# Attention on one core: transposing the weights of two units in a row, head 0's mixes at fixed places, a later v, and an earlier logarithm

## The chip, the cores and the metric

The kernel runs on one core of one Trainium2 chip. The metric is the device time of one execution in microseconds; before the change the median of three runs is 965.65 us (965.34 to 966.77). The engines are named as in the profile: PE is TensorE, with PEld for its weight loads; DVE is VectorE, ACT is ScalarE, POOL is GpSimd, SP is SyncE, which only issues DMAs here.

## What is computed

One layer of a decoder: 1,024 tokens of width 1,024, in float32. A norm, one wide projection, then two groups of heads side by side: eight heads of differential softmax attention and four of gated linear attention (GLA); their outputs are gated, multiplied by the output weights, normed and added to the input. The change touches the attention heads:

```python
s = jnp.einsum('bqhmd,bkhmd->bhmqk', qb, k)     # two maps m per head, 64 wide
p = jax.nn.softmax(jnp.where(mask, s, -jnp.inf), axis=-1)
w = p[:, :, 0] - lam * p[:, :, 1]
out = jnp.einsum('bhqk,bkhv->bqhv', w, v)
...
oa = rms_norm(oa, subln_g) * (1.0 - lam_init)
oa = oa.reshape(B, S, DA_WIDTH) * jax.nn.silu(ga)
```

## The kernel before, in words

Products in float32 are made of three matmuls on values split in a high and a low part (hi·hi, lo·hi, hi·lo); a cast on ACT gives the high part and a subtraction on DVE the low one. The program has three parts. Up to about 617 us stand the projections and GLA. From there to about 925 us comes attention. Then the finishing part adds up the output, norms it and stores it.

Attention is three streams of work, written as generators that `merge` (L1203) interleaves by costs written down in the code. All matmuls and transpositions are recorded by `mm` (L141, its instruction on L142) and `tr` (L144, L145) with `keep_in_program_order`, so the merged order is TensorE's order. The instructions of the other engines all carry L66, a helper; their order in each queue is chosen by the compiler's scheduler, unless an instruction is kept in program order or told to be issued after another (`issue_after`). A queue runs strictly in its order.

- `all_scores` (L1330) goes over the heads, and in a head over the query blocks qb from 7 down to 0, each of 128 queries and (qb+1)·128 keys. `scores` (L1263) does a block: for each map m, PE writes scores into one of three PSUM banks `sc` (up to 512 keys a part, two matmuls each: k and ks); DVE adds the mask, copies the part into the tile p and keeps the row's lowest (a reduction, CUSTOM_DVE_ANT_0, and an accumulator read); when a map's parts are in, ACT takes the exponential of the whole row and its sum. After both maps DVE takes the two reciprocals at once, POOL scales map 1 by lam and its reciprocal, and DVE mixes the two maps into p0 (SCALAR_TENSOR_TENSOR). That mix is the weight block. p0 of each block has a place of its own; p1 has two buffers for all of them, in the pool `smp`. In head 0 the mixes of blocks 7 to 4 are put off: a list holds them until the next block's second map is reduced.
- `all_values` (L1424) goes over units (head, half, keys): ten a head. `turn` (L1350) makes three or four transpositions of 128x128 into one of two PSUM banks `wtr` and takes the result out, ACT as `wt_hi`, DVE as `wt_lo` (three buffers each). `weigh` (L1366) multiplies with v into the bank `po`. Turns run two units ahead of weighs. After each half, `attn_norm` (L1380) norms the 128x512 output `o` and gates it: the squares, a matmul with ones (`ms`), logarithm and exponential on ACT, `r`; in head 7 the result `gate` stays on the chip for the end.
- `out_early` (L1528) makes the output's products that don't depend on what is still missing (`ypart`, three matmuls of 512 columns a step) and so fills TensorE between the other two.

`load_qk` (L1118) and `load_v` (L1238) issue DMAs on SP. Head 0's v is loaded ahead of the stream, by `v_first` (L1248), so the tile v has the first memory of `smp`. The projections store q and k with DMAs `q_d<-qk_st` (L482) from memory that `smp` takes over. At the end, `early_ends` (L1622) uses head 7's last gate: `last_part` (L1505) splits it into `m_hi` and `m_lo`, and `mix_pair` (L1612) had split the parts before (`m_raw`) behind the last square sums (`squared_last`).

Of the kernel before, what the change touches and what calls it, by code (L numbers as in the profile page):

```python
# [10 lines left out]
AF = mybir.ActivationFunctionType  # L11
# [9 lines left out]
DA_HEADS = 8  # L21
# [10 lines left out]
def hymba_kernel(  # L32
# [21 lines left out]
    pe, sp = nc.tensor, nc.sync  # L54
# [20 lines left out]
    act, dve, pool = Queue(nc.scalar), Queue(nc.vector), Queue(nc.gpsimd)  # L75

    def fp(t):
        return t.bitcast(F32)
# [37 lines left out]
    v_d = [tc.dram_tile([4, 2, P, NT, P], F32, name=f"v{u}_d") for u in range(2)]  # L116
# [1121 lines left out]
    def load_v(h):  # L1238
        v = [smp.tile([P, NT, P], F32R, tag="v", name=f"v{t}", bufs=4) for t in range(2)]
        for t in range(2):  # L1240

            with tc.issue_after(qk_load[0]) if h else nullcontext():
                ins = sp.dma_start(fp(v[t]), v_d[h // 4][h % 4, t])
            if h == 0:
                tc.keep_in_program_order(ins)
        return v

    v_first = load_v(0)  # L1248

    n_sc, n_tr = [0], [0]  # L1250

# [11 lines left out]
    def scores(h, qb):  # L1263

        n = (qb + 1) * P
        qc = slice(qb % 4 * P, qb % 4 * P + P)
        st = const.tile([P, 6], F32, tag="stt", name="stt", bufs=4)
        p0 = pp.tile([P, n], F32, tag=f"p0_{qb}", name="p0", bufs=1 + (qb > 5))
        p1 = smp.tile([P, S], F32, tag="p1", name="p1", bufs=2)
        for m, p in enumerate((p0, p1)):  # L1270
            q = qk[h, "q", qb // 4][:, m, qc]
            parts = parts_of(n)
            if h == DA_HEADS - 1 and (qb, m) in ((1, 1), (0, 0), (0, 1)):

                parts = [(0, 512)]
            for i, (a, b) in enumerate(parts):
                sc = sc_bank("sc", [P, 512])
                for j, name in enumerate(("k", "ks")):
                    for half in range(2):
                        lo, hi = max(a, half * 512), min(b, half * 512 + 512)  # L1280
                        if lo < hi:
                            mm(
                                sc[:, lo - a : hi - a], q,
                                qk[h, name, half][:, m, lo - half * 512 : hi - half * 512],
                                start=(j == 0), stop=(j == 1),
                            )
                e = min(b, n)
                last = i == len(parts) - 1

                behind = tc.issue_after(lowest[0]) if (h, qb) == (0, NT - 2) else nullcontext()  # L1290
                with behind:
                    ins = dve.tensor_tensor_reduce(
                        p[:, a:e], sc[:, : e - a],
                        maskt[:, NZ + P - (e - a) :] if last else maskt[:, : e - a],
                        1.0, 3e38 if i == 0 else st[:, 4 + m : 5 + m], ALU.add, ALU.min,
                        st[:, m : m + 1] if last else st[:, 4 + m : 5 + m],
                    )
                if (h, qb) == (0, NT - 1):
                    lowest[:] = [ins.ins]
                c = 0.08 + (e - a) / 512 * 0.56  # L1300
                if last:
                    act.activation(
                        p[:, :n], p[:, :n], AF.Exp, bias=st[:, m : m + 1], scale=-1.0,
                        accum_out=st[:, 2 + m : 3 + m],
                    )
                if last and m:
                    dve.reciprocal(st[:, 4:6], st[:, 2:4])
                    pool.tensor_scalar(
                        p1[:, :n], p1[:, :n], st[:, 5:6], lam, ALU.mult, ALU.mult
                    )  # L1310
                    while mixed:
                        with tc.issue_after(ins.ins):
                            mixed.pop()()

                    def mix_maps():
                        dve.scalar_tensor_tensor(
                            p0[:, :n], p0[:, :n], st[:, 4:5], p1[:, :n], ALU.mult, ALU.subtract
                        )
                        w[h, qb] = p0

                    if h == 0 and qb > 3:
                        mixed.append(mix_maps)
                    else:
                        mix_maps()
                    c += 0.25 + n / 1024 * 1.4
                yield c

    lowest, mixed = [], []

    def all_scores():  # L1330
        for h in range(DA_HEADS):
            for qb in range(NT - 1, -1, -1):
                if qb in (3, 5) and h:
                    yield lambda h=h, half=qb // 4: (h - 1, half) in used
                yield from scores(h, qb)
                if qb == 4 and h + 1 < DA_HEADS:
                    for n in ("q", "k", "ks"):
                        load_qk(h + 1, n, 1)
                    for n in ("k", "ks"):
                        load_qk(h + 1, n, 0)  # L1340
            if h + 1 < DA_HEADS:
                load_qk(h + 1, "q", 0)
        scored.append(True)
        opened.update(dict.fromkeys(SC))
# [5 lines left out]
    def turn(h, half, kts):  # L1350

        pt = tr_bank("wtr", [P, 512])
        n = 0
        for kt in kts:
            for i in blocks_of(kt, half):
                tr(pt[:, n : n + P], w[h, 4 * half + i][:, kt * P : (kt + 1) * P])
                n += P
        hi = smp.tile([P, 512], F32R, tag="wt_hi", name="wt_hi", bufs=3)
        lo = smp.tile([P, 512], F32R, tag="wt_lo", name="wt_lo", bufs=3)
        turned_last[:] = [act.copy(hi[:, :n], pt[:, :n]).ins]  # L1360
        dve.tensor_tensor(lo[:, :n], pt[:, :n], fp(hi[:, :n]), ALU.subtract)
        return hi, lo
# [14 lines left out]
                )  # L1377
            n += ns

    def attn_norm(h, half, o):  # L1380
        if h < DA_HEADS - 1:
            gate = smp.tile([P, 512], F32, tag="gate", name="gate", bufs=2)
        else:
# [10 lines left out]
        with tc.issue_after(turned_last[0]) if ending else nullcontext():  # L1394
            act.activation(sq[:64], o[:64], AF.Square)
        dve.tensor_tensor(sq[:64], sq[:64], fold[:64], ALU.add)
        ins = act.copy(hl[:64], sq[:64]).ins
        if ending:
            squared_last.append(ins)
        dve.tensor_tensor(hl[64:], sq[:64], fp(hl[:64]), ALU.subtract)  # L1400
        if h == DA_HEADS - 1:

# [7 lines left out]
            opened[TR[n_tr[0] % 2]] = None  # L1410
        r = smp.tile([P, 512], F32, tag="r", name="r", bufs=1)
        act.activation(r, ms, AF.Ln, bias=eps_t, scale=1.0 / P)
        act.activation(r, r, AF.Exp, scale=-0.5)
        if h < DA_HEADS - 1:
            dve.scalar_tensor_tensor(r, o, sub_g, r, ALU.mult, ALU.mult)
            pool.tensor_tensor(gate, r, gate, ALU.mult)
# [7 lines left out]
    def all_values():  # L1424


        AHEAD = 2
        units = [
            (h, half, kts) for h in range(DA_HEADS) for half in (1, 0)
            for kts in [(k,) for k in range(4 * half + 2)] + [(4 * half + 2, 4 * half + 3)]  # L1430
        ]
        vs, os, turned, norms_todo = {0: v_first}, {}, {}, []
        ahead = iter(units)

        def norm_step():
            while norms_todo:
                c = next(norms_todo[0], None)
                if c is not None:
                    return
                norms_todo.pop(0)  # L1440

        for i, (h, half, kts) in enumerate(units):
            last = kts[-1] == 4 * half + 3

            ahead_by = AHEAD if h < DA_HEADS - 1 else AHEAD
            while len(turned) < min(i + 1 + ahead_by, len(units)):
                u = next(ahead)
                if u[2] == (0,):
                    yield lambda: (u[0], 4 * u[1]) in w
                turned[u] = turn(*u)  # L1450
                if u[2][-1] == 4 * u[1] + 3:
                    used.add(u[:2])
                yield 0.4
                norm_step()
            if kts == (0,):
                o = smp.tile([P, 512], F32, tag="o", name="o", bufs=3)
                po = bank(PO, [P, 512], "po")
            weigh(po, half, kts, vs[h], turned[h, half, kts])
            norm_step()
            if last:  # L1460
                act.copy(o, po)
                if half and h + 1 < DA_HEADS:
                    vs[h + 1] = load_v(h + 1)
                norms_todo.append(attn_norm(h, half, o))
            yield 0.6

            if i == 1:
                yield SOON * DA_HEADS * 10.0 / T
        carry = norms_todo[-1]
        while len(norms_todo) > 1:  # L1470
            norm_step()
        next(carry)
        yield 0.0
        yield lambda: (ENDS[2], 0) in ps_d
        early_ends()
        yield from carry
# [319 lines left out]
```

## Time and profile before

| what | value |
|---|---|
| median of three runs | 965.65 us (965.34 to 966.77) |
| the profiled execution's own time | 964.64 us |
| its span, first to last instruction | 962.9 us |
| busy: PE, DVE, ACT, POOL | 953.0, 736.6, 603.6, 199.0 us |
| granted TensorE clock, mean | 0.998 |
| transpositions `wtr` | 288, busy 44.5 us |
| DMA | 220.36 MB, mean 229 GB/s |

Busy time is the share of time in which an engine had an instruction under way. Matmuls overlap, and their recorded ends are modelled, so what one costs TensorE is read between the starts of two in a row, not from its duration. In a timeline the columns are start, duration, engine, line, operation, output <- inputs, shapes, the count of equal instructions in the row, and in brackets how long the engine stood idle before it and what ended that.

### The profile page before, as it was taken

How to read it: one execution, taken by the hardware profiler on the slowest of the kernel's cores; microseconds unless marked ns; L12 is line 12 of the kernel's file. 1: busy time of each engine (PE TensorE's matmuls, PEld its weight loads, DVE VectorE, ACT ScalarE, POOL GpSimd, SP SyncE). 2: the span in 40 equal slices, each digit the busy share in tenths (PEclk: the TensorE clock that was granted, in tenths of full speed). 3: DMA queues.
4: the chain of work that ended last, by engine and by line, in shares of the span. 5: the costliest groups of instructions: out<-in, count | busy, mean ns of one | idle time of the engine just before them, and what ended most of it. 6: DMA issues, size and time to landing. Idle time of an engine off the chain costs nothing.

```text
span 962.9 us, 14404 instructions
## 1 busy us (share of the span) xinstructions
PE 953.0 (99%) x4640; PEld 795.9 (83%) x4640; DVE 736.6 (76%) x1468; ACT 603.6 (63%) x1166; POOL 199.0 (21%) x264
## 2 busy tenths in 40 slices
PE   9999999999999999999999999999999999999997
PEld 7887788888888888888888888878888888888875
DVE  5898799996678687687667576587888888898554
ACT  8753355845677556577765344366777787787773
POOL 3101002122142112111100002122222222433321
PEclk9999999999999999999999999999999999999999
DMA  9616367487577897985754498996666669994767
GB/s 343 217 35 167 91 196 253 163 299 246 189 251 239 281 309 236 299 285 193 259 175 145 151 291 273 408 305 198 219 207 208 220 226 357 320 292 104 162 196 149
DMA packets 152827, 220.36 MB, mean 229 GB/s; under 512 B 15728, under 2 KB 85360, under 8 KB 152656
## 3 DMA queue, kind: packets, MB, share of 16 engines
q1 hardware_dynamic: 138304, 177.65, 57.5%
q0 software_dynamic: 14448, 41.79, 14.9%
q8 instruction: 37, 0.61, 0.3%
q14 instruction: 38, 0.31, 0.1%
HBM read 133.93 MB, written 88.60 MB: 231 GB/s over the span
## 4 chain that ended last, share of the span: by engine, by line
PE 96%; ACT 1%; DVE 1%; DMA 1%; issue 0%; SPq 0%; DVEq 0%; ACTq 0%
PE x L142 24%; PE y L142 16%; PE z L142 16%; PE ypart L142 13%; PE sc L142 7%; PE po L142 5%; PE yps L142 4%; PE wtr L145 3%; PE gpo L142 3%; PE kv L142 1%; PE gkl_ps L142 1%; PE pa L142 1%; DMA x<-in_x_dram 1%; PE xT L145 1%; DVE p L66 1%
## 5 line engine op out<-in xcount | busy, mean ns | idle before, releaser
L66 ACT CAST w<-w_raw 128x512 fp32r<-128x512 f32 x138 | 85.2, 621 | 76.8 <-PE y L142 33.6
L66 DVE TENSOR_TENSOR w<-w_raw,w 128x512 fp32r<-128x512 f32 x138 | 94.1, 685 | 38.4 <-ACT w L66 38.2
L66 ACT ACTIVATE p<-p,stt 128x896 f32<-128x896 f32 (+7 forms) x128 | 99.3, 776 | 34.3 <-DVE stt L66 33.0
L66 ACT COPY s<-x 128x512 f32<-128x512 f32 x78 | 44.8, 587 | 74.2 <-PE x L142 74.0
L66 DVE CUSTOM_DVE_ANT_0 p<-sc,maskt 128x512 f32<-128x512 f32 (+3 forms) x128 | 74.3, 585 | 16.0 <-PE sc L142 14.6
L66 POOL TENSOR_SCALAR p<-p,stt,lam 128x1024 f32<-128x1024 f32 (+3 forms) x64 | 56.4, 882 | 144.8 <-DVE stt L66 144.1
L142 PE MATMUL z<-s_hi,w 128*128 128x512 f32 x320 | 80.2, 393 | 0.0
L142 PE MATMUL x<-s_hi,w 128*128 128x512 f32 x320 | 80.1, 392 | 0.0
L142 PE MATMUL y<-h_hi,w 128*128 128x512 f32 x320 | 80.1, 392 | 0.0
L142 PE MATMUL ypart<-wo_hi,m_hi 128*128 128x512 f32 x192 | 79.5, 414 | 0.1
L142 PE MATMUL ypart<-wo_hi,m_lo 128*128 128x512 f32 x192 | 75.5, 393 | 0.0
L142 PE MATMUL ypart<-wo_lo,m_hi 128*128 128x512 f32 x192 | 75.4, 393 | 0.0
L66 POOL DMA_DIRECT2D wo_d<-wo_hi x32 | 17.4, 544 | 275.0 <-ACT wo_hi L66 275.0
L142 PEld LDWEIGHTS z<-s_hi,w 128*128 128x128 f32 x320 | 59.8, 188 | 12.4
L142 PEld LDWEIGHTS x<-s_hi,w 128*128 128x128 f32 x320 | 59.7, 188 | 12.4
L142 PEld LDWEIGHTS y<-h_hi,w 128*128 128x128 f32 x320 | 59.7, 188 | 12.3
L142 PE MATMUL sc<-k,q 128*128 128x512 f32 (+1 forms) x192 | 68.7, 362 | 0.6 <-DVE stt L66 0.6
L142 PE MATMUL sc<-ks,q 128*128 128x512 f32 (+1 forms) x192 | 66.1, 347 | 0.0
L66 ACT CAST wt_hi<-wtr 128x512 fp32r<-128x512 f32 (+1 forms) x80 | 42.8, 535 | 27.1 <-PE wtr L145 26.1
L66 DVE TENSOR_TENSOR wt_lo<-wtr,wt_hi 128x512 fp32r<-128x512 f32 (+1 forms) x80 | 50.6, 632 | 9.0 <-ACT wt_hi L66 8.5
L66 DVE TENSOR_TENSOR w_raw<-w_raw 128x512 f32<-128x512 f32 x80 | 55.2, 690 | 1.2 <-DMA w_raw<-in_w_in_dram 0.2
L66 DVE TENSOR_TENSOR c<-z,s 128x512 f32<-128x512 f32 x48 | 32.8, 687 | 29.8 <-ACT s L66 19.9
(232 smaller groups left out, 2352.0 us busy)
## 6 DMA issues: line engine op xcount, KB each, us to landing
w_raw<-in_w_in_dram SPq DMA_DIRECT2D x40, 512.0 KB, 5.0
wo_d<-wo_hi POOLq DMA_DIRECT2D x32, 256.0 KB, 3.3
q<-q_d SPq DMA_DIRECT2D x32, 256.0 KB, 4.8
k<-k_d SPq DMA_DIRECT2D x32, 256.0 KB, 5.4
ks<-k_d SPq DMA_DIRECT2D x64, 128.0 KB, 5.9
v<-v_d SPq DMA_DIRECT2D x16, 512.0 KB, 6.5
wo_raw<-in_w_out_dram POOLq DMA_DIRECT2D x31, 256.0 KB, 4.8
wo_d<-gqd POOLq DMA_DIRECT2D x22, 256.0 KB, 4.2
```

The costliest lines, as they stand in the source:

```text
L66: ins = op(*a, **k)
L142: tc.keep_in_program_order(pe.matmul(*a, **k))
L145: tc.keep_in_program_order(pe.transpose(dst, src, ident))
```

## The change

It has five parts, all in attention.

1. **Turns in pairs.** `turn` only transposes; the take-out is a function of its own, `take_out`. `all_values` takes two units at a time and transposes both in a row. The second is taken out at once, unless it is the third ahead (`late`): then it is taken out behind the weigh of unit i. So of 80 runs of three or four transpositions come 40 runs of six to eight.
2. **Head 0's mixes at fixed places.** The list `mixed` becomes a table: the mix of block 7 stands behind the reduction of (5, map 0), 6 behind (4, 0), 5 behind (4, 1), 4 behind (3, 1), 3 behind (1, 0), 2 behind (0, 0). Head 0's reductions are kept in program order on DVE.
3. **Head 0's v** is loaded in the stream, behind the q of head 1, no longer ahead of it.
4. **The last copy of `o`** (head 7, first half) stands behind the exponential of the norm before it.
5. **The end's logarithm.** `squared_last` is now the exponential of the norm of head 7's second half, not the cast of its squares. What is issued after it (the casts of `m_raw`) therefore stands behind that logarithm and exponential.

```diff
-            with tc.issue_after(qk_load[0]) if h else nullcontext():
-                ins = sp.dma_start(fp(v[t]), v_d[h // 4][h % 4, t])
-            if h == 0:
-                tc.keep_in_program_order(ins)
+            with tc.issue_after(qk_load[0]):
+                sp.dma_start(fp(v[t]), v_d[h // 4][h % 4, t])
...
-    v_first = load_v(0)
...
+                if h == 0:
+                    tc.keep_in_program_order(ins)
                 c = 0.08 + (e - a) / 512 * 0.56
+                if last and (qb, m) in mixed:
+                    with tc.issue_after(ins.ins):
+                        mixed.pop((qb, m))()
...
-                    while mixed:
-                        with tc.issue_after(ins.ins):
-                            mixed.pop()()
...
-                    if h == 0 and qb > 3:
-                        mixed.append(mix_maps)
+                    if h == 0 and qb > 1:
+                        mixed[(qb - 1, 1) if qb in (4, 5) else (qb - 2, 0)] = mix_maps
...
-                    for n in ("q", "k", "ks"):
+                    load_qk(h + 1, "q", 1)
+                    if not h:
+                        vs[0] = load_v(0)
+                    for n in ("k", "ks"):
                         load_qk(h + 1, n, 1)
...
+        return pt, n
+
+    def take_out(pt, n):
+
         hi = smp.tile([P, 512], F32R, tag="wt_hi", name="wt_hi", bufs=3)
         lo = smp.tile([P, 512], F32R, tag="wt_lo", name="wt_lo", bufs=3)
...
-    def attn_norm(h, half, o):
+    def attn_norm(h, half, o, po):
+        if h == DA_HEADS - 1 and not half:
+            with tc.issue_after(squared_last[0]):
+                act.copy(o, po)
...
-        ins = act.copy(hl[:64], sq[:64]).ins
-        if ending:
-            squared_last.append(ins)
+        act.copy(hl[:64], sq[:64])
...
-        act.activation(r, r, AF.Exp, scale=-0.5)
+        ins = act.activation(r, r, AF.Exp, scale=-0.5).ins
+        if ending:
+            squared_last.append(ins)
...
-            ahead_by = AHEAD if h < DA_HEADS - 1 else AHEAD
-            while len(turned) < min(i + 1 + ahead_by, len(units)):
-                u = next(ahead)
-                if u[2] == (0,):
-                    yield lambda: (u[0], 4 * u[1]) in w
-                turned[u] = turn(*u)
-                if u[2][-1] == 4 * u[1] + 3:
-                    used.add(u[:2])
-                yield 0.4
+            late = None
+            while len(turned) < min(i + 3, len(units)):
+                pair = [next(ahead), next(ahead)]
+                for u in pair:
+                    if u[2] == (0,):
+                        yield lambda: (u[0], 4 * u[1]) in w
+                pts = [turn(*u) for u in pair]
+                for u, pt in zip(pair, pts):
+                    if len(turned) == i + 3:
+                        late, turned[u] = (u, pt), None
+                    else:
+                        turned[u] = take_out(*pt)
+                    if u[2][-1] == 4 * u[1] + 3:
+                        used.add(u[:2])
+                yield 0.8
+                norm_step()
                 norm_step()
...
             weigh(po, half, kts, vs[h], turned[h, half, kts])
+            if late:
+                turned[late[0]] = take_out(*late[1])
             norm_step()
             if last:
-                act.copy(o, po)
+                if i + 1 < len(units):
+                    act.copy(o, po)
```

What this does to DVE's queue in head 0 is seen where the reductions of block 7 end and those of block 6 begin. Before (ISA with two inputs is a reduction of one part, ISA on 128x1 its accumulator read, p_5863 is block 7's map 1, p_5897 and p_5898 block 6's two maps; in brackets stand the semaphores that a row waits for):

```order
L66 ISA p_5863,stt<-sc,maskt,stt 128x512 [waits DVE_49,PE_49]
L66 ISA stt 128x1
L66 ISA p_5897,stt<-sc,maskt 128x512 [waits PE_49]
L66 ISA stt 128x1
L66 ISA p_5897,stt<-sc,maskt,stt 128x384 [waits DVE_49,PE_49]
L66 ISA stt 128x1
L66 RECIPROCAL stt<-stt 128x2 [waits Activation_49]
L66 ISA p_5898,stt<-sc,maskt 128x512 [waits PE_49]
```

And now, at the same place (block 7's map 1 is p_5859, block 6's maps are p_5893 and p_5894):

```order
L66 ISA p_5859,stt<-sc,maskt,stt 128x512 [waits DVE_49,PE_49]
L66 ISA stt 128x1
L66 RECIPROCAL stt<-stt 128x2 [waits Activation_49]
L66 ISA p_5893,stt<-sc,maskt 128x512 [waits PE_49]
L66 ISA stt 128x1
L66 ISA p_5893,stt<-sc,maskt,stt 128x384 [waits DVE_49,PE_49]
L66 ISA stt 128x1
L66 ISA p_5894,stt<-sc,maskt 128x512 [waits DMAHW3_49,DMAHW2_49,DMAHW4_49,DMAHW1_49,PE_49]
L66 ISA stt 128x1
L66 ISA p_5894,stt<-sc,maskt,stt 128x384 [waits DVE_49,PE_49]
L66 ISA stt 128x1
L66 RECIPROCAL stt<-stt 128x2 [waits Activation_49]
```

The reciprocal of a block, which waits for ACT, has moved from behind the next block's first map to a place ahead of it, and the same holds for blocks 6, 5, 4 and 3. The first part of block 6's map 1 waits for four DMA queues more: p1's second buffer now lies where v lay, in memory that the last stores of q (`q_d<-qk_st`) still read.

At the end ACT's queue changes too. Before, from the cast of the last square sums of head 7's second half (`sq_hl`) on:

```order
L66 CAST sq_hl<-sq 64x512
L66 COPY yps<-yp 128x512 x2
L66 CAST m_hi<-m_raw 128x384 x2
L66 COPY yps<-yp 128x512
L66 COPY o<-po 128x512
L66 ACTIVATE r<-ms,eps_t 128x512
L66 ACTIVATE fold<-o 64x512
L66 ACTIVATE r<-r 128x512
L66 ACTIVATE sq<-o 64x512
L66 CAST m_hi<-gate 128x128 x2
```

And now:

```order
L66 CAST sq_hl<-sq 64x512
L66 COPY yps<-yp 128x512 x2
L66 ACTIVATE r<-ms,eps_t 128x512
L66 ACTIVATE r<-r 128x512
L66 COPY o<-po 128x512
L66 CAST m_hi<-m_raw 128x384 x2
L66 COPY yps<-yp 128x512
L66 ACTIVATE fold<-o 64x512
L66 ACTIVATE sq<-o 64x512
L66 CAST m_hi<-gate 128x128 x2
```

The logarithm (`r<-ms`) and the exponential (`r<-r`) have moved ahead of two casts and two copies; `m_hi<-gate`, which the output's last matmuls need, still stands behind all of them.

More of the change, by code (lines that the diff above doesn't have):

```diff
@@ L1326, in scores @@
                 yield c
-    lowest, mixed = [], []
+    lowest, mixed, vs = [], {}, {}
     def all_scores():
@@ L1424, in all_values @@
     def all_values():
-        AHEAD = 2
         units = [
@@ L1431, in all_values @@
         ]
-        vs, os, turned, norms_todo = {0: v_first}, {}, {}, []
+        os, turned, norms_todo = {}, {}, []
         ahead = iter(units)
@@ L1458, in all_values @@
             weigh(po, half, kts, vs[h], turned[h, half, kts])
+            if late:
+                turned[late[0]] = take_out(*late[1])
             norm_step()
             if last:
-                act.copy(o, po)
+                if i + 1 < len(units):
+                    act.copy(o, po)
                 if half and h + 1 < DA_HEADS:
                     vs[h + 1] = load_v(h + 1)
-                norms_todo.append(attn_norm(h, half, o))
+                norms_todo.append(attn_norm(h, half, o, po))
             yield 0.6
```

## The prediction

> **What bounds the kernel now.** I read the page's chain of waits first, then busy time by stretches, then the timelines of PE, DVE and ACT where head 0 begins and where attention ends. The chain by engine:
>
> ```profile
> PE 96%; ACT 1%; DVE 1%; DMA 1%; issue 0%; SPq 0%; DVEq 0%; ACTq 0%
> ```
>
> The time is TensorE's work and the places where it stands. Two stretches of attention, with the busy time of PE, PEld, DVE, ACT and POOL, then clock, DMA share and GB/s:
>
> ```profile
> 600.00:645.00 45.00, 43.87 (x205) 35.53 (x204) 31.15 (x82) 22.24 (x48) 10.60 (x15) 1.00 1.00 359
> 645.00:890.00 245.00, 245.00 (x1311) 208.48 (x1310) 206.94 (x560) 185.17 (x402) 72.86 (x79) 1.00 0.74 238
> ```
>
> From 645 to 890 us TensorE never stands, so nothing that only hastens DVE or ACT there can gain. It stands in head 0 (45.00 − 43.87 = 1.13 us idle) and at the end. Head 0 on PE:
>
> ```profile
> 631.16 0.40 PE L142 MATMUL sc<-ks,q 128*128 128x512 f32 x1
> 631.80 0.33 PE L142 MATMUL sc<-k,q 128*128 128x128 f32 x1 [0.24 <-DVE stt L66]
> ...
> 637.72 0.66 PE L145 MATMUL wtr<-ident,p 128*128 128x128 f32 x4 [0.40 <-DVE p L66]
> ...
> 646.56 0.39 PE L142 MATMUL sc<-k,q 128*128 128x512 f32 x1
> ```
>
> Scores wait for DVE to empty one of three banks, the first transpositions for DVE's mix of block 4. So DVE sets the pace of this stage. Its queue, and ACT's:
>
> ```profile
> 623.50 0.69 DVE L66 CUSTOM_DVE_ANT_0 p<-sc,maskt 128x512 f32<-128x512 f32 x1 [0.44 <-PE sc L142]
> ...
> 624.97 0.67 DVE L66 CUSTOM_DVE_ANT_0 p<-sc,maskt 128x512 f32<-128x512 f32 x1
> ...
> 626.57 1.28 DVE L66 SCALAR_TENSOR_TENSOR p<-p,stt,p 128x1024 f32<-128x1024 f32 x1
> 627.77 0.68 DVE L66 CUSTOM_DVE_ANT_0 p<-sc,maskt 128x512 f32<-128x512 f32 x1
> ...
> 631.05 0.69 DVE L66 CUSTOM_DVE_ANT_0 p<-sc,maskt 128x512 f32<-128x512 f32 x1
> ```
>
> ```profile
> 623.10 1.15 ACT L66 ACTIVATE p<-p,stt 128x1024 f32<-128x1024 f32 x1 [0.27 <-DVE stt L66]
> 624.15 0.19 ACT L66 ACTIVATION_READ_ACCUMULATOR p<-p,stt 128x1 f32 x1
> ```
>
> Block 7's second exponential ends at 624.15 + 0.19 = 624.34. DVE did not wait for it: block 6's first reduction began at 623.50.
>
> **Part by part: head 0's order (the largest term).** The reciprocals now stand ahead of the next block's first reduction, so DVE, whose queue is strict, waits each time for ACT's exponential with everything queued behind. I walk DVE's new order, with reductions of 0.61 from start to start on 512 columns and 0.3 to 0.5 on fewer, mixes of at most 1.28 and exponentials of at most 1.15, shorter with each block as its rows get shorter.
>
> - Block 6, map 0: reciprocal at 624.37, reduction at 624.45 instead of 623.50, 0.95 late.
> - Block 6, map 1: this reduction now also waits for the last stores of q that read its memory:
>
> ```profile
> L482 SPq DMA_DIRECT2D q_d<-qk_st x1: 446/446/446, 621.5 to 621.5; - x1
> ...
> DMA to landing us min/median/max: 5.2/5.2/5.2
> ```
>
>   They land at 621.5 + 5.2 = 626.7; the reduction stood at 624.97. So it comes 1.8 late.
> - Block 5, map 0: behind block 6's two reductions (1.2) stand an exponential of 1.05, its read and the reciprocal (together 1.5): 626.8 + 1.2 + 1.5 = 629.5 instead of 627.77. Still 1.8 late, since block 7's mix (1.28) went behind this place.
> - Block 4, map 0: four reductions (2.0), that mix (1.2 from start to start) and a naked exponential with read and reciprocal (1.4), with 0.3 of waiting between: 634.5 instead of 631.05, 3.4 late. Before, the same stretch held four reductions and one mix with no exponential, 3.3.
> - The next two stretches go the same way, but block 4's exponential hides behind block 5's mix, so nothing is added. Block 4's mix, shortened to 640 columns, runs from 640.2 to 641.05, and the first transpositions start at 641.1 instead of 637.72, 3.4 late.
> - Block 1's mix waits for POOL and now stands ahead of block 0's first reduction. That keeps a score bank closed until 647.4; the last score matmuls of head 1's first block start at 650.8, where the row says 646.56. Up to there TensorE has done the same work in both orders: **4.2 late**. Behind it stands the stretch without idle time, where nothing can be won back.
>
> Without the DMA's wait the walk gives 0.95 less, without POOL's hold 1.5 less, so 1.75 to 4.8 (the landing up to 0.6 later). The later v sits ahead of head 1's keys in SP's queue:
>
> ```profile
> v<-v_d SPq DMA_DIRECT2D x16, 512.0 KB, 6.5
> ```
>
> Issued behind head 1's q it holds these keys back; by the walk they land near 646.6, just when TensorE comes for them. I price it at 0, and at up to 0.5 in the range.
>
> **Pairs of turns.** What a run costs TensorE is read between starts:
>
> ```profile
> 649.53 0.60 PE L145 MATMUL wtr<-ident,p 128*128 128x128 f32 x4
> 649.89 0.48 PE L142 MATMUL ypart<-wo_hi,m_hi 128*128 128x512 f32 x1
> 650.20 0.39 PE L142 MATMUL ypart<-wo_hi,m_lo 128*128 128x512 f32 x1
> 650.43 0.40 PE L142 MATMUL ypart<-wo_lo,m_hi 128*128 128x512 f32 x1
> ```
>
> From 649.53 to 650.20 pass 0.67 us, of which one matmul of 512 columns takes 0.23 (650.20 to 650.43): 0.44 for four, 0.11 each, though one lasts 0.60 − 3·0.11 = 0.27. Ends of a run thus cost next to nothing, and 40 joined pairs save 0 to 0.3; I take **−0.1**. [...]
>
> The second take-out of a pair now waits for the weigh of the unit two before, which frees its `wt` buffer, and must be through before its PSUM bank is transposed into again. Counted along TensorE's new order at 0.23 a matmul, that leaves, of 38 places, 1.9 us at two, 2.6 at five, 2.7 to 2.8 at three and 2.9 to 4.4 at the others. It needs:
>
> ```profile
> L66 ACT ACTIVATE p<-p,stt 128x896 f32<-128x896 f32 (+7 forms) x128 | 99.3, 776 | 34.3 <-DVE stt L66 33.0
> ...
> L66 ACT CAST wt_hi<-wtr 128x512 fp32r<-128x512 f32 (+1 forms) x80 | 42.8, 535 | 27.1 <-PE wtr L145 26.1
> L66 DVE TENSOR_TENSOR wt_lo<-wtr,wt_hi 128x512 fp32r<-128x512 f32 (+1 forms) x80 | 50.6, 632 | 9.0 <-ACT wt_hi L66 8.5
> ```
>
> 0.54 + 0.63 = 1.2, and with one exponential ahead of it in ACT's queue (0.78) 1.95: two places overrun, by 0.1 in all. With two ahead, 2.73: seven do, by 2.5. I take **+0.8**, between them and nearer the first, because ACT is busy 185 of 245 us here; range 0 to 2.5.
>
> **The end.** PE waits twice for head 7's last gate; ACT's queue ahead of it:
>
> ```profile
> 912.61 0.50 PE L142 MATMUL ms<-sq_hl,ones 128*128 128x512 f32 x1
> ...
> 917.54 0.39 PE L142 MATMUL yps<-wo_lo,m_hi 128*128 128x512 f32 x1
> 918.23 0.50 PE L142 MATMUL yps<-wo_hi,m_hi 128*128 128x512 f32 x1 [0.30 <-ACT m_hi L66]
> 918.97 0.50 PE L142 MATMUL yps<-wo_hi,m_lo 128*128 128x512 f32 x1 [0.23 <-DVE m_lo L66]
> ```
>
> ```profile
> 912.78 0.92 ACT L66 CAST m_hi<-m_raw 128x384 fp32r<-128x384 f32 x2
> ...
> 917.36 0.63 ACT L66 ACTIVATE sq<-o 64x512 f32<-64x512 f32 x1 [0.76 <-DVE gate L66]
> ```
>
> ACT does the same work ahead of `m_hi` in either order. Logarithm and exponential first, the gate is ready early and the 0.76 of idle goes; but the logarithm, now in the place of the casts at 912.78, waits 0.3 for its matmul `ms` (912.61 + 0.50 = 913.1). `m_hi` and `m_lo` come 0.5 earlier, and so does PE: **−0.5**. Bounds: all of both waits, 918.97 − 917.54 − 2·0.23 = 0.97, and +0.2 if the casts of `m_raw`, now later, hold DVE's `m_lo`. The moved copy of `o` is one of those steps.
>
> **Sum.** 4.2 − 0.1 + 0.8 − 0.5 = +4.4 us. On the profiled execution's 964.64 that is 969.0; the median of 965.65 lies 1.0 above it, so **970.0**.
>
> **The rivals.** *Head 0 hardly late (0.14).* The stores of q land before 624.5 and POOL's hold ends before PE comes: 1.75 at the start, pairs 0, the end −0.5, the sum +1.1: 966.8, no change. For it speaks that the landing is one execution's; against it that the issue at 621.5 precedes 624.97 by only 3.5 us.
>
> *Faster: ends of runs cost (0.01).* If TensorE paid 0.27 − 0.11 = 0.16 at the end of each run, 40 joined pairs would give 6.5 back: 4.5 − 6.5 = −2.0, 963.6. The rows from 649.53 on speak against it.
>
> *Faster: head 0's waits go (0.04).* If ACT has finished each exponential when DVE reaches the reciprocal, the fixed mixes only bring blocks 7 to 4 to their transpositions sooner. PE's idle 1.13, with 0.17 for each of five refills (631.16 to 631.80 is 0.64, 0.41 above the usual 0.23, for 0.24 idle), makes 2.0; with the end and the pairs −2.6: 963.0. It decides at one point: block 7's exponential must end before 623.50. The row says 624.34.
>
> *Late take-outs bind (0.09).* Two exponentials and a DVE instruction of 0.6 ahead of each, 3.3: most windows overrun, by 10.7 together. That makes 4.2 − 0.1 + 10.7 − 0.5 = +14.3, 980.0. Against it: ACT is idle a quarter of that stretch.
>
> **How the numbers follow.** The forecast has 0.72, the rivals 0.14, 0.01, 0.04 and 0.09, in the order told. A measurement of this kernel tells 0.2%, 1.9 us, from no change: 963.7 to 967.6. So slower 0.72 + 0.09 = 0.81, same 0.14, faster 0.05. The range goes from 966.3, the no-change rival with the end's whole bound (1.75 − 0.1 − 0.97), to 973.0, the forecast with 4.8 + 0.5 at the start and 2.5 for the take-outs (7.2 above 965.65, rounded up). It leaves out the faster rivals and the slowest, 0.14.
>
> **What would show it.** In the profile after: DVE idle before RECIPROCAL, released by ACT, at blocks 7 to 4; the reduction of block 6's map 1 released by a DMA; PE's waits in head 0 longer and named DVE; the first transpositions of `wtr` three to four us later; ACT's `r<-ms` right behind `ms` and PE's two waits at 918 shorter by 0.5. From head 2 on, no wait on `wtr`'s bank beyond a few tenths. I am wrong if the first transpositions start within 1 us of 637.72, or if head 2 and later show TensorE waiting for `wt_hi` or `wt_lo`.

## The result, and the profile after

The changed kernel takes 982.34 us (median of five runs, 978.52 to 982.45) against 965.65 us: ratio 1.0157, 95% interval 1.0137 to 1.0177. By the medians that is 16.7 us slower; the ratio, which weighs all five runs, makes it 15.2. The forecast was 4.4, and 973.0 was the range's end. Three of the five runs lie at 982.3 to 982.5 with a mean clock of 0.995 to 0.996, two at 978.5 and 978.9 with 0.998; the profiled one, with a span of 980.6 us, is one of the three.

The chain of waits of the changed kernel, by engine; PE had 96% of it:

```profile
PE 81%; DVE 7%; DMA 5%; SPq 3%; ACT 2%; issue 2%; DVEq 0%; POOL 0%; ACTq 0%
```

Where TensorE stands shows in the busy times by stretches (PE, PEld, DVE, ACT, POOL, then clock, DMA share, GB/s):

```profile
600.00:655.00 55.00, 50.54 (x223) 39.84 (x223) 34.52 (x91) 24.52 (x51) 10.23 (x15) 0.97 0.92 332
...
800.00:850.00 50.00, 45.08 (x230) 37.48 (x229) 39.00 (x98) 33.52 (x71) 15.57 (x16) 0.97 0.99 337
```

Before, TensorE stood for 1.1 us from 600 to 645 and never from 645 to 890. Now it stands 4.5 us in head 0 and 4.9 us between 800 and 850 us, around the norms of the fourth and fifth heads, and in both stretches the granted clock is 0.97. TensorE waiting for `wt_lo` behind head 2 was the prediction's own sign of being wrong.

Head 0 in the changed kernel, on DVE and on PE:

```profile
624.93 0.17 DVE L66 RECIPROCAL stt<-stt 128x2 f32<-128x2 f32 x1 [1.36 <-ACT p L66]
625.01 0.67 DVE L66 CUSTOM_DVE_ANT_0 p<-sc,maskt 128x512 f32<-128x512 f32 x1
...
627.20 0.69 DVE L66 CUSTOM_DVE_ANT_0 p<-sc,maskt 128x512 f32<-128x512 f32 x1 [0.74 <-DMA q_d<-qk_st]
...
629.92 0.17 DVE L66 RECIPROCAL stt<-stt 128x2 f32<-128x2 f32 x1 [1.25 <-ACT p L66]
630.00 0.67 DVE L66 CUSTOM_DVE_ANT_0 p<-sc,maskt 128x512 f32<-128x512 f32 x1
...
635.15 0.17 DVE L66 RECIPROCAL stt<-stt 128x2 f32<-128x2 f32 x1 [1.16 <-ACT p L66]
635.24 0.67 DVE L66 CUSTOM_DVE_ANT_0 p<-sc,maskt 128x512 f32<-128x512 f32 x1
```

```profile
630.74 0.39 PE L142 MATMUL sc<-k,q 128*128 128x256 f32 x1 [1.28 <-DVE stt L66]
...
635.97 0.33 PE L142 MATMUL sc<-k,q 128*128 128x128 f32 x1 [1.19 <-DVE stt L66]
...
642.96 1.03 PE L145 MATMUL wtr<-ident,p 128*128 128x128 f32 x8
```

Up to here this is the walk of the prediction. The whole profile is 0.5 us later already at 617 us, ahead of anything changed. With that taken off, the first reductions of blocks 6, 5 and 4 start at 624.5, 629.5 and 634.7 (forecast 624.45, 629.5, 634.5), and the DMA of q's stores holds the second map's to 626.7 (626.8). The first transpositions come 4.7 us late, where 3.4 were forecast; an estimated 1.6 of that is a lower clock, shown below. Then block 1's mix waits for POOL and keeps a score bank closed, as the prediction said:

```profile
649.50 0.48 DVE L66 SCALAR_TENSOR_TENSOR p<-p,stt,p 128x256 f32<-128x256 f32 x1 [0.69 <-POOL p L66]
```

```profile
650.25 0.50 PE L142 MATMUL sc<-k,q 128*128 128x512 f32 x1 [1.09 <-DVE stt L66]
```

What the prediction missed comes 200 us later. Where the longest wait is, PE and DVE of the changed kernel read:

```profile
840.22 0.33 PE L142 MATMUL sc<-ks,q 128*128 128x384 f32 x1
843.51 0.47 PE L142 MATMUL ms<-sq_hl,ones 128*128 128x512 f32 x1 [2.96 <-DVE wt_lo L66]
```

```profile
839.10 1.09 DVE L66 TENSOR_TENSOR m_lo<-m_raw,m_hi 128x512 fp32r<-128x512 f32 x1 [0.23 <-ACT m_hi L66]
840.11 1.27 DVE L66 SCALAR_TENSOR_TENSOR p<-p,stt,p 128x1024 f32<-128x1024 f32 x1
841.42 0.69 DVE L66 TENSOR_TENSOR sq_hl<-sq,sq_hl 64x512 fp32r<-64x512 f32 x1
842.14 0.62 DVE L66 CUSTOM_DVE_ANT_0 p<-sc,maskt,stt 128x384 f32<-128x384 f32 x1
...
842.68 0.68 DVE L66 TENSOR_TENSOR wt_lo<-wtr,wt_hi 128x512 fp32r<-128x512 f32 x1
```

The norm's matmul `ms` takes the bank that the first run of a pair has just filled. The take-out of that run isn't the late one. ACT has done its half of it at 840.07, but DVE comes to the other half only at 842.68, behind a mix, `sq_hl` and a reduction.

The other long wait is for a late take-out. TensorE needs the bank at 806.01, 2.06 us after the end of the weigh that lets the take-out go (803.56 + 0.39). On PE, ACT and DVE:

```profile
803.56 0.39 PE L142 MATMUL po<-wt_lo,v 128*128 128x512 f32 x1
...
807.89 0.99 PE L145 MATMUL wtr<-ident,p 128*128 128x128 f32 x7 [1.88 <-DVE wt_lo L66]
```

```profile
804.64 0.62 ACT L66 CAST m_hi<-m_raw 128x512 fp32r<-128x512 f32 x1 [3.88 <-DMA m_raw<-mixd]
805.17 1.04 ACT L66 ACTIVATE p<-p,stt 128x896 f32<-128x896 f32 x1
...
806.21 0.67 ACT L66 ACTIVATE r<-ms,eps_t 128x512 f32<-128x512 f32 x1
806.78 0.47 ACT L66 CAST wt_hi<-wtr 128x384 fp32r<-128x384 f32 x1
```

```profile
807.27 0.56 DVE L66 TENSOR_TENSOR wt_lo<-wtr,wt_hi 128x384 fp32r<-128x384 f32 x1 [0.75 <-ACT wt_hi L66]
```

It isn't the weigh that this take-out waits for in the end. Ahead of it in ACT's queue stand a cast that waits 3.88 us for a load, an exponential and a logarithm.

Behind the long wait and behind head 0's waits TensorE's granted clock is 0.50 for 3.41 us. Here are two stretches for each place, the one before and the low one; the clock is the value behind the five busy times:

```profile
633.01:636.42 3.41, 1.69 (x8) 1.05 (x8) 1.97 (x10) 1.03 (x2) 0.98 (x1) 1.00 0.38 111
636.42:639.83 3.41, 3.41 (x9) 2.62 (x9) 3.05 (x6) 1.83 (x4) 0.00 (x0) 0.50 0.50 141
...
841.22:844.63 3.41, 1.12 (x5) 0.98 (x6) 3.20 (x8) 1.75 (x4) 0.00 (x0) 1.00 1.03 347
844.63:848.04 3.41, 3.41 (x10) 2.62 (x9) 1.57 (x5) 2.00 (x5) 1.56 (x2) 0.50 1.08 354
```

In the low stretches matmuls of 512 columns start 0.427 us apart (six steps from 636.62 to 639.18, three from 846.54 to 847.82) instead of 0.23, by which an estimated 1.6 us are lost each time (3.41·(1 − 0.23/0.427)).

### The profile page after: what moved, and what is told of

It is laid out like the page before. It is cut to its first block, busy times and chain, and to the rows that moved or that the text cites. A ratio compares the mean times of both kernels' runs of the same rounds, so it can differ in the third digit from the quotient of the medians.

```text
span 980.6 us, 14433 instructions
## 1 busy us (share of the span) xinstructions
PE 958.8 (98%) x4640; PEld 798.2 (81%) x4640; DVE 740.5 (76%) x1468; ACT 602.7 (61%) x1166; POOL 199.8 (20%) x264
## 4 chain that ended last, share of the span: by engine, by line
PE 81%; DVE 7%; DMA 5%; SPq 3%; ACT 2%; issue 2%; DVEq 0%; POOL 0%; ACTq 0%
PE x L142 20%; PE z L142 14%; PE y L142 14%; PE ypart L142 10%; PE sc L142 5%; PE po L142 5%; PE yps L142 4%; PE gpo L142 3%; PE wtr L145 2%; DMA g_raw<-in_w_in_dram 2%; DVE p L66 2%; PE kv L142 1%; DMA k_d<-qk_st 1%; ACT p L66 1%; DVE s_lo L66 1%
## 5 line engine op out<-in xcount | busy, mean ns | idle before, releaser
L142 PEld LDWEIGHTS x<-s_hi,w 128*128 128x128 f32 x320 | 59.7, 188 | 12.4
L142 PEld LDWEIGHTS y<-h_hi,w 128*128 128x128 f32 x320 | 59.7, 188 | 12.3
L66 DVE TENSOR_TENSOR wt_lo<-wtr,wt_hi 128x512 fp32r<-128x512 f32 (+1 forms) x80 | 50.4, 633 | 16.7 <-ACT wt_hi L66 15.6
L66 DVE SCALAR_TENSOR_TENSOR p<-p,stt,p 128x1024 f32<-128x1024 f32 (+4 forms) x64 | 53.7, 839 | 3.3 <-POOL p L66 3.1
```

The lines of the kernel that those rows point to most:

```text
L66: ins = op(*a, **k)
L142: tc.keep_in_program_order(pe.matmul(*a, **k))
```

## The experiments

Two theories went in. A: three separate costs, head 0, the late take-outs and the end, each with its own place. B: one cause, head 0's delay, that puts the loads and casts of later heads out of step.

**Each part alone on the kernel before.** Head 0's part (the mixes, the program order, the later v):

> The kernel before with only head 0's part of the change: the mixes at fixed places, the reductions in program order, v behind head 1's q. Theory A (three separate costs: head 0 about 4.5 us of DVE waiting for ACT plus 1.9 us of lowered TensorE clock behind it, the late take-outs about 7 plus 1.8 of lowered clock, the end about 1): +4.5 to +6.5 us, 970 to 972, with the waits of 630 to 650 us as in the changed kernel and no wait of TensorE between 660 and 890. Theory B (one cause: head 0's delay pushes loads and casts of the later heads out of step, so that the waits at 805 and 840 us follow from it): +12 or more, with waits at 805 and 840.

Measured: 968.84 against 964.58, ratio 1.0047 (1.0032 to 1.0062), +4.3 us. There is no wait over 0.2 us between 660 and 890 us, so theory B is out. The prediction's 4.2 lies in the interval, +3.1 to +6.0; theory A's +4.5 had counted a lowered clock, which this profile doesn't have (its mean clock is 0.999). In the profile TensorE comes to the first transpositions and to the last score matmul of head 1's first block at these times:

```profile
641.23 0.66 PE L145 MATMUL wtr<-ident,p 128*128 128x128 f32 x4
...
650.06 0.40 PE L142 MATMUL sc<-k,q 128*128 128x512 f32 x1
```

Before they stood at 637.72 and 646.56, so both are 3.5 us late (3.8 if one adds that this profile is 0.3 ahead at 617 us). The first was forecast 3.4 late, the second 4.2: the 0.8 between them, POOL's hold of block 1's mix, doesn't occur here.

Turns in pairs alone:

```diff
-                turned[u] = turn(*u)
...
+                pts = [turn(*u) for u in pair]
+                for u, pt in zip(pair, pts):
+                    if len(turned) == i + 3:
+                        late, turned[u] = (u, pt), None
...
             weigh(po, half, kts, vs[h], turned[h, half, kts])
+            if late:
+                turned[late[0]] = take_out(*late[1])
```

> The kernel before with only the turns in pairs and the late take-out. Theory A: +7 to +10 us, 973 to 976: TensorE waits for wt_lo at two or three places between 700 and 890 us, one of them over 2 us, and ACT's queue waits for po. Theory B: less than +3, no single wait over 1 us between 660 and 890.

Measured: 976.85 against 964.58, ratio 1.0128 (1.0113 to 1.0144), +12.3 us: more than theory A's 10, and three quarters of the whole loss. The waits of PE and of ACT in this run (us in total, times, longest):

```profile
PE ms L142 <- DVE wt_lo L66: 3.3, 2, 2.9
PE wtr L145 <- DVE wt_lo L66: 2.8, 3, 1.7
```

```profile
ACT wt_hi L66 <- PE po L142: 17.2, 15, 3.9
```

ACT stands 17.2 us in 15 places in front of a late take-out, waiting for TensorE's weigh. This line is new. But 12.4 of the 17.2 us lie between 655 and 780 us, and there TensorE waits once, for 0.67 us. Its two longest waits, 1.68 at 801.36 and 2.94 at 837.01, come where ACT has no such wait (775 to 838 us). The first is the one shown above, behind a cast that waited 3.69 us for its load, the second that of `ms`. The longer one is accompanied and followed by 6.8 us with a clock of 0.50:

```profile
836.30:839.71 3.41, 2.70 (x6) 2.15 (x7) 2.33 (x7) 2.86 (x6) 0.00 (x0) 0.50 1.07 327
839.71:843.13 3.42, 3.42 (x10) 2.65 (x9) 0.92 (x3) 1.18 (x3) 2.35 (x2) 0.50 1.05 408
```

The end's two edits alone:

> The kernel before with only the end's two edits (the last copy of o and the casts of m_raw behind the exponential). The prediction's term: -0.5 us, 965.1, the two waits of TensorE at 918 us (0.46 and 0.51 between starts) down to about 0.5 together. The other view, that the end's edits themselves cost what the changed kernel loses there: +0.5 to +1.5.

Measured: 964.41 against 964.58, ratio 0.9997 (0.9988 to 1.0006), no difference that can be told. At the end of attention PE in this run reads:

```profile
916.08 0.39 PE L142 MATMUL yps<-wo_lo,m_hi 128*128 128x512 f32 x1
916.92 0.50 PE L142 MATMUL yps<-wo_hi,m_hi 128*128 128x512 f32 x1 [0.46 <-ACT yps L66]
917.26 0.39 PE L142 MATMUL yps<-wo_hi,m_lo 128*128 128x512 f32 x1
```

The two waits for the gate are gone, and one for ACT's copy `yps` has come, which now stands behind the logarithm and exponential: 0.84 − 0.23 = 0.6 between starts beyond a matmul's own, where 0.46 + 0.51 were. So 0.35 of the forecast 0.5.

**Head 0: which detail.** With v loaded first as before:

> As head 0's part alone, but v is loaded first as before, so that the second buffer of p1 doesn't lie in memory that the stores of q still read. If the walk of DVE's queue is right, 0.95 us less than with the later v plus what the lowered clock took: +3 to +4, 968.7 to 969.7. If the DMA's wait is what makes the stage late, no more than +1.5. If the reciprocals' places alone do it, the same as with the later v within 0.5.

Measured: 967.34, ratio 1.0036 (1.0021 to 1.0050), +2.8, at the foot of the +3 to +4 that were expected. By the medians the later v, through the DMA's wait, costs the remaining 1.5, but the two intervals overlap. In the two profiles, whose instructions stand in the same order on every engine, the score matmul shown above starts at 650.06 and 649.25; counted from each profile's own time at 617 us the later v costs 1.0, and 0.95 was forecast. With v first and the reductions not kept in order (against the run before):

```diff
-                if h == 0:
-                    tc.keep_in_program_order(ins)
```

> Head 0's mixes at the new fixed places with v loaded first and the reductions not kept in program order: the reciprocals then stand behind the next block's first reduction again. If the reciprocals' places are what costs (the prediction's step), 964.6 within 1 us of the kernel before. If the fixed places of the mixes cost by themselves, the same +2.8 as with the reductions kept in order.

Measured: 965.22 against 965.04, ratio 1.0003 (0.9993 to 1.0012). The fixed places of the mixes cost nothing that can be told; the program order, which forces the reciprocals ahead of the next block's reductions, costs the 2.8.

**Pairs: the bank or the wait.** From the profile I had a second theory, M: `ms` needs the bank of a pair's first run 1.7 to 2.8 us after it was filled, once a head, by TensorE's order at 0.23 us a matmul, where it had at least 3.0 before. Against it stood L, that the late take-out's wait for the weigh is what costs. A score bank for `ms`:

```diff
+        if h < DA_HEADS - 1:
+            ms = sc_bank("ms", [P, 512])
...
```

> Pairs alone, but the norm's matmul ms of heads 0 to 6 writes into the next score bank, so that it doesn't need a bank of the pair. Theory M: the waits of ms for wt_lo at about 834 us and the lowered clock behind it are gone, +4 to +7 remain (the late take-out at 799, head 0, the end). Theory L: +10 or more, waits for wt_lo elsewhere. New waits of scores for the borrowed bank, if any, up to 1 us.

Measured: 979.30, ratio 1.0145 (1.0128 to 1.0162), +14.3, worse than the pairs as they are. In the place where `ms` had waited for `wt_lo`, it now waits 2.3 us for DVE's reductions, and in four more places it waits for the borrowed bank (up to 1 us was expected):

```profile
PE ms L142 <- DVE stt L66: 5.4, 5, 2.3
PE wtr L145 <- DVE wt_lo L66: 3.6, 3, 2.6
```

So at that place it is DVE's queue that is late, whichever bank `ms` takes. As a test of theory M as a whole the run is weak, since the borrowed bank brought waits of its own. The late take-out without pairs, single turns in their old places, two buffers:

```diff
-        hi = smp.tile([P, 512], F32R, tag="wt_hi", name="wt_hi", bufs=3)
-        lo = smp.tile([P, 512], F32R, tag="wt_lo", name="wt_lo", bufs=3)
...
+        hi = smp.tile([P, 512], F32R, tag="wt_hi", name="wt_hi", bufs=2)
+        lo = smp.tile([P, 512], F32R, tag="wt_lo", name="wt_lo", bufs=2)
...
+                if len(turned) == i + 2:
+                    late, turned[u] = (u, pt), None
```

> The kernel before with single turns in their old places, but each take-out that is two units ahead stands behind the weigh and, with two wt buffers, has to wait for it: the late take-out without the pairs. Theory L: +6 or more, TensorE waiting for wt_lo. Theory M: ms keeps its 3.2 us and more; +3 at most.

Measured: 978.72, ratio 1.0144 (1.0128 to 1.0159), +13.7. And the same with three buffers, TensorE's order unchanged:

> The single late take-out again, with three wt buffers instead of two and TensorE's order the same word for word: the take-out still stands behind the weigh in the program, but its buffer is free, so nothing in ACT's or DVE's queue waits for TensorE. If the wait for the weigh is what costs (ACT 37.9 us of waiting for po in the run with two buffers): within 1.5 us of the kernel before. If it is the later place in the program or the order of the queues: still +8 or more.

Measured: 964.24 against 965.01, ratio 0.9992 (0.9983 to 1.0001). With two buffers, ACT and PE:

```profile
ACT wt_hi L66 <- PE po L142: 37.9, 29, 3.5
```

```profile
PE wtr L145 <- DVE wt_lo L66: 8.4, 11, 1.4
```

ACT with three:

```profile
ACT wt_hi L66 <- PE wtr L145: 25.9, 26, 3.4
```

With three, ACT waits for transpositions, as before the change, and TensorE never for `wt_lo`. With two, ACT stands before the weigh, and TensorE waits for `wt_lo` eleven times ahead of a run of transpositions. Each time the take-out it waits for is that of the bank it needs next. One of these places, on PE, ACT and DVE:

```profile
875.24 0.39 PE L142 MATMUL po<-wt_lo,v 128*128 128x512 f32 x1
...
878.03 0.52 PE L145 MATMUL wtr<-ident,p 128*128 128x128 f32 x3 [1.36 <-DVE wt_lo L66]
```

```profile
875.86 0.59 ACT L66 CAST wt_hi<-wtr 128x512 fp32r<-128x512 f32 x1
```

```profile
876.06 0.69 DVE L66 TENSOR_TENSOR m_lo<-m_raw,m_hi 128x512 fp32r<-128x512 f32 x1
876.66 0.61 DVE L66 CUSTOM_DVE_ANT_0 p<-sc,maskt,stt 128x384 f32<-128x384 f32 x1
...
877.20 0.69 DVE L66 TENSOR_TENSOR wt_lo<-wtr,wt_hi 128x512 fp32r<-128x512 f32 x1
```

From the weigh's end (875.63) to the bank's next use (878.03 − 1.36 = 876.67) there is 1.04 us, in the eleven places 0.7 to 1.7. The take-out alone needs 1.2, and casts, reductions or a logarithm stand ahead of it. So here the windows are too short.

The two programs differ in one buffer, and TensorE's order is the same. The order of ACT's and DVE's queues is not: with three buffers the scheduler left them almost as in the kernel before, with two it moved instructions in some 80 places on ACT and 100 on DVE. What the wait costs by itself and what the new order costs is therefore not separated. A run that keeps these orders and only opens the buffer is missing.

**How much of the pairs is the wait.** Pairs with four buffers, so that nothing waits for a weigh, with room taken from `gate` and `o`:

> Pairs alone, but with four wt_hi/wt_lo buffers, so that both take-outs of a pair stand at once behind their transpositions and none waits for a weigh (room made by one buffer for gate and two for o). Theory L (the loss of the pairs is the late take-out's wait for the weigh): most of the 12.3 us gone, at most +3. Theory M (the loss is that the norm's matmul ms now needs the bank of the pair's first run 1.7 to 2.8 us after it was filled, where it had at least 3.2 before, plus the lowered clock that follows the longest wait): still +6 or more, with a wait of ms for wt_lo.

Measured: 971.21, ratio 1.0064 (1.0048 to 1.0079), +6.2. Its control, the kernel before with only that room taken:

> The kernel before with one buffer for gate and two for o and nothing else: what the room for four wt buffers cost in the run of pairs with four buffers. Within 0.5 us of the kernel before if these buffers had no part in its +6.2; +2 or more if they explain a third of it or more.

Measured: 968.97, ratio 1.0034 (1.0020 to 1.0048), +4.0: the first answer was spoiled. POOL's waits in the control, from 640 to 905 us, say why:

```profile
POOL gate L66 <- DMA gate<-g_d: 27.0, 4, 8.0
```

With one buffer POOL stands up to 8 us for the gate's load, and its scaling of map 1 behind that; DVE's waits for POOL rise from 2.4 to 8.8 us. So the room was taken from `o` and `m_raw` instead:

> Pairs with four wt buffers again, with the room taken from o (two buffers) and m_raw (three) and gate as before, since the single gate buffer made POOL wait 27 us for loads in the run that took it away. If the late take-out's wait is nearly all that the pairs cost: +0 to +2.5. If joining the runs and moving TensorE's other work around them costs by itself: +4 or more, with waits of TensorE for wt_lo at about 830 us.

> The kernel before with only that room taken: two buffers for o and three for m_raw. Within 0.5 us of the kernel before if gate's buffer alone was the cost of the first control; +2 or more if o's or m_raw's buffers cost too.

Measured: the control 964.86, ratio 1.0003 (0.9993 to 1.0012), which is clean; the pairs 969.31, ratio 1.0050 (1.0036 to 1.0063), +4.7. TensorE's order is that of the pairs alone. So of the 12.3 us the late take-outs cost 7.6, with the places that the scheduler gave ACT's and DVE's other work around them and with the lower clock behind `ms` (an estimated 2.8 in the one profile there is, by the same starts). The joined runs themselves, with TensorE's other work moved around them, cost 4.7. PE's waits in the latter, from 617 us on, begin:

```profile
PE ms L142 <- DVE wt_lo L66: 1.7, 1, 1.7
PE wtr L145 <- DVE wt_lo L66: 1.1, 2, 0.7
PE ms L142 <- DVE sq_hl L66: 0.9, 1, 0.9
PE po L142 <- ACT o L66: 0.7, 1, 0.7
...
```

Of these 4.4 us 2.8 are waits for a bank that a run has just filled: `ms` 1.7 in one place, the next runs 1.1 right behind the first run of eight. So theory M has a part here. The other 1.6 are for `ms`' own input and for the copy of `o`; why they come with the joined runs is not shown.

**The change without its two costly details** (v first, reductions free, four buffers), with either room:

> The whole change with its two costly details taken out: v loaded first and head 0's reductions not kept in program order, and four wt buffers so that no take-out waits for a weigh. If the costs add up as the runs so far say (0.2 + 6.2 - 0.2): +6, 971. If the two details are all there is: within 1.5 us of the kernel before. If pairs with four buffers only looked better because head 0 was as before: +10 or more.

> The whole change with v first, head 0's reductions free and four wt buffers by that room. If the two details are all that the change costs: within 2 us of the kernel before. If the joined runs cost as well: what the run of pairs with the same room costs, less 0.2 for the end, +4 or more.

Measured: 973.34 with the single gate buffer, ratio 1.0081 (1.0066 to 1.0096), +8.3, where the sum of the parts was +6; 970.26 with the other room, ratio 1.0059 (1.0045 to 1.0073), +5.6, where it was 4.5. The second view is right: the joined runs cost as well. But both are 1 to 2 us above their sums, so the parts are not quite independent; the profile of the first has 2.8 us of waits for score banks, which the pairs with that room had for 0.4. The parts of the change itself, 4.3 + 12.3 − 0.2 = 16.4, come near its 16.7.

**A version that beats both?** The two pieces that measured below the kernel before, together:

> The kernel before with the two pieces that measured below it, the take-out behind the weigh with three buffers (-0.8) and the end's two edits (-0.2): if both are real, -1.0, 0.999 of the time before, at the edge of what a measurement tells; if the first was scatter, no difference.

Measured: 965.00 against 964.61, ratio 1.0002 (0.9993 to 1.0011). There was nothing in them; no version here beats the kernel before.

## Why the prediction was wrong

- **The late take-out**: this is the step that failed. It was priced at +0.8, with 2.5 as its bound; with TensorE's order kept, the late take-outs cost 7.6 in the pairs and 13.7 with single turns. The question, whether each is through before its own bank is needed, was a right one, and the windows were right: at 807.89 the bank was needed 2.06 us after the weigh, where 1.9 was the shortest on the list. What failed is the count of what stands ahead. The prediction put 1.2 us of work and one exponential there, two at most, all on ACT. The rows show a cast held 3.88 us by a load, an exponential and a logarithm on ACT, and with single turns casts and reductions on DVE. It took the order of the other queues as given, too, where the scheduler makes a new one around an instruction that has to wait. How much of the 7.6 is the wait and how much the new order stays open.
- **Who needs a bank next**: the list held only the late take-outs. The longest wait, 2.96 us, is for the take-out of a pair's first run: `ms` comes 1.7 to 2.8 us behind that run and wasn't on the list. That part stays when no take-out is late (1.7 of the joined runs' 4.7).
- **The clock** had no term. The profile before shows 1.00 from 600 to 890 us, and the forecast let waits cost their own length. In the changed kernel's profile two low stretches, 3.41 us at 0.50, cost an estimated 1.6 us each.
- **The rival with 980.0 us** and a chance of 0.09 had the right part and its mechanism, windows that overrun. That its time comes near is luck: it let most windows overrun, for 10.7 us, and the profile shows one late take-out that does, for 1.88. ACT's idle quarter, given against it, was no argument, since part of that idle time was ACT standing before a load or a weigh with its queue behind it.
- **Head 0's order**: forecast 4.2, alone 4.3, and the walk holds nearly in each time. The agreement to 0.1 is in part luck: in that run's profile the stage ends 3.5 to 3.8 us late, without POOL's hold, for which the walk had 0.8. In the whole change the hold is there (0.69 us on DVE, 1.09 on TensorE). The two causes were forecast at 3.25 and 0.95 and measured at 2.8 and 1.5 by the medians, the second at 1.0 in the profiles. The later v's delay of head 1's keys, priced at 0, made no wait that the runs show.
- **Joined runs on TensorE**: forecast −0.1. What a run costs TensorE was read rightly: in the changed kernel a run of seven at 656.28 costs 0.77 us between its neighbours, 0.11 each, as before. That joining would cost 4.7 through DVE and ACT was not in the sum.
- **The end**: forecast −0.5, seen −0.35 in its own waits, since the copy `yps` was pushed back by the same edit; the time itself shows no difference.

Together: between the two profiles the span grows by 17.7 us. TensorE's waits from 617 us on grow by 11.0 (1.5 to 12.5), the two low stretches take 3.2, and 0.5 was there before 617 us; the remaining 3 were not followed up.

## What to carry to other kernels

When an edit moves a take-out behind something, list for its bank who needs it next and how long after the release, and list all that stands ahead of the take-out in both queues, not the exponentials alone: a cast that waits for a load closes the queue as well (3.88 us here). Then look again at the order that the scheduler makes: with TensorE's order unchanged, one buffer decided between +13.7 us and nothing, and the other queues were reordered with it. And run a control for the room that an experiment takes: here a single gate buffer cost +4.0, nearly as much as the joined runs that the experiment was to measure.

## What the runs showed of the hardware

- In the changed kernel's attention the granted clock is 0.50 in two stretches of 3.41 us, from 636.42 and from 844.63, both behind waits of TensorE. They begin 208.21 us apart, which is 61.0 times the 3.413 us that the trace records for each. In the pairs alone it is 0.50 for 6.8 us, from 836.30. The sum of the waits alone doesn't tell when: head 0's four waits, 3.0 us of idle together, were followed by a low stretch in the changed kernel, and the run with head 0's part alone, where TensorE waits 3.3 us in five places for DVE's reductions, has a mean clock of 0.999; one stretch of 3.41 us at 0.50 would by itself make that 0.998. The run with `ms` in a score bank has a wait of 2.56 us (to 806.47), and its clock from 806 to 812 is 1.00.
- How close together the idle time lay differs in these cases. In the 3.41 us ahead of the changed kernel's two low stretches TensorE stood 1.72 and 2.29 us (3.41 − 1.69 and 3.41 − 1.12 in the rows above); in the pairs alone 2.23 of the wait's 2.94 us lie ahead of the low stretch. The 1.88 us wait at 807.89, cut at whole steps of 3.413 from 636.42, falls into two of them, 1.07 us of idle from 803.67 and 0.81 from 807.08, and the clock is 1.00 in both. Idle time is counted from a matmul's recorded end to the next start, and the recorded ends are modelled. From how much idle time on the clock falls is not shown by so few cases.
- Transpositions of 128x128 in a row start 0.11 us apart, though the record of one lasts 0.27: the run of eight at 642.96 lasts 1.03 us, 0.27 + 7·0.109, and seven cost TensorE 0.77 us between their neighbours, four 0.44. In these rows one of seven costs the same 0.11 as one of four, so joining runs had nothing to save on TensorE.
